# One transformer layer on one NeuronCore: the first steps in a hand-written order

## The chip, the core and the metric

The kernel runs on one core of a Trainium2 chip. The core has five engines that run their own instruction queues, each in order: TensorE (PE in the profile, with its weight loads as PEld), VectorE (DVE), ScalarE (ACT), GpSimd (POOL, here "Pool") and SyncE (SP), which here only starts transfers. They wait for each other with semaphores. The metric is the device time of one execution in microseconds (us); less is better.

## What is computed

One decoder layer for 256 tokens of width 1024, all float32. The input is normalised; one combined projection `w_in` feeds an RWKV-7 branch, a block-sparse attention branch and the gates; the branches are merged, projected, and a gated feed-forward part with a short convolution follows.

```python
h = rms_norm(x, norm1_g[l])
proj = h @ w_in[l]
z_rwkv = z_rwkv + rwkv_mu[l] * (shift_right(z_rwkv) - z_rwkv)
y_a = rwkv7_time_mix(z_rwkv, ...)
q = partial_rope(rms_norm(q, q_norm_g[l]), positions)
y_b = moba_attention(q, k, v)
x = x + (g_a * u_a + g_b * u_b) @ w_out[l]
x = x + conv_ffn(h2, w_ffn_up[l], ffn_conv_w[l], ffn_conv_b[l], w_ffn_down[l])
```

Only the first lines matter here: `rms_norm`, the first columns of `w_in` and what the first transfers bring.

## The kernel before

**Products in two parts.** Every float32 matrix is split in a high part, rounded to a format in which TensorE takes one pass (float32r), and the low rest. A product is high x high + high x low + low x high, three passes. For the weights, `load_next` (L234) starts the transfer of a block of 128 x 1024 numbers into one of four `raw` buffers, `split_hi` (L246 on ScalarE, L248 on VectorE) makes `whi` in one of four buffers, and `split_lo` (L256, VectorE) makes `wlo` in one of three and, since `raw` is then free, calls `load_next` for the next block. `wst` (L284 to L289) consumes a block: for each of two column halves eight products with `whi` (with hh and hl in turn) and four with `wlo`. For the activations hh and hl are the same two parts of the normalised input, turned so that the channels lie on the partitions.

**Who sets the order.** Instructions are written in program order, and a scheduler places those of each engine by its own estimate of when their data are there, so an instruction can stand far ahead of its place in the text. Two things bind it: `issue_after` (after a named instruction), and, in the changed kernel, `manual_schedule` (the instructions of the named engines keep the written order among themselves). Within an engine the built order is fixed: an instruction that waits holds up all behind it. Transfers are started from two queues, SP's and Pool's; each has a small number of completion semaphores that it uses in turn, so that a transfer can also wait for an earlier one of its queue.

**The first steps.** SP starts four loads of `x` (two row blocks, two halves), four weight blocks, then the ten small loads of `p1` (L397), then reloads of `raw`. Pool starts the load of `norm1_g`, makes `jp` (column minus row) and from it `ident`, the unit matrix, then starts ten small loads (`wdu`, `wgu`, `gqk`, the positions `posi`, the convolution's parameters). TensorE runs eleven products on constants so as not to start idle (`keep_warm`, L99). For each row block `norm_t` squares and sums the two halves on ScalarE (`part`, L326), takes the root (L333) and the reciprocal (L335), multiplies the rows by it into `xn` (`first`, L336 to L340), and turns them on TensorE by a product with `ident` (`turn`, L352). `second` scales with `norm1_g`, which stands in the columns of `par`, and makes hh (L357, ScalarE) and hl (L358, VectorE) for each of eight channel blocks; hh of the two blocks that share a PSUM bank are made one after the other. VectorE makes the first weight block's high part, ScalarE and VectorE the next ones.

**What follows.** The first projection (256 columns, two weight blocks) gives `xwa` and half of `xg`, a narrow one the rest. `shift` (L426 on ScalarE, L427 on VectorE) mixes each column with its predecessor, with the parameters `omm` and `par`. ScalarE takes tanh and sigmoid of them, TensorE multiplies `xwa` with `wdu` (`ch`, L494) into PSUM banks, three of which are kept for this chain, and ScalarE makes `sg` and `av`. VectorE sums `sg` along the sequence (`L`, L507, with the constant `rst`), ScalarE takes two exponentials, squares the projected keys (`sq`, L523), and TensorE sums the squares (`pss`, L529); the reciprocal roots are spread (`rx`, L536) and turned (`prx`, L546). VectorE then makes the operands of the chunk products `pgr` (L592), whose results it masks into G (L595) with `gmask`. Next to this chain run the other projections; `SLACK` and the pairs that the generators yield decide in program order how chain and projections are interleaved. `late_consts` makes the masks and other constants on VectorE, `late_params` turns the parameters `p1` and `p2` into columns, `rope_tables` makes sine and cosine of the positions (`posf`, L204, to `trig`, L225).

## Time and profile before

| | us |
|---|---|
| median of 3 runs (438.62 to 439.71) | 438.62 |
| the profiled execution | 438.61 |
| its span from first to last instruction | 436.8 |
| TensorE busy | 425.6 |
| VectorE busy | 301.4 |
| ScalarE busy | 243.0 |
| Pool busy | 12.8 |

The 1.8 us between time and span lie before the first and behind the last instruction. A row of the profile's timeline gives the start, the duration, the engine, the line, the operation, what it writes and reads, and in brackets how long the engine was idle before and what ended that. Rows of several instructions (xN) span from the first to the last. The durations of TensorE's products overlap, so their starts tell its pace.

### The profile page before, as it was taken

How to read it: one execution, taken by the hardware profiler on the slowest of the kernel's cores; microseconds unless marked ns; L12 is line 12 of the kernel's file. 1: busy time of each engine (PE TensorE's matmuls, PEld its weight loads, DVE VectorE, ACT ScalarE, POOL GpSimd, SP SyncE). 2: the span in 40 equal slices, each digit the busy share in tenths (PEclk: the TensorE clock that was granted, in tenths of full speed). 3: DMA queues.
4: the chain of work that ended last, by engine and by line, in shares of the span. 5: the costliest groups of instructions: out<-in, count | busy, mean ns of one | idle time of the engine just before them, and what ended most of it. 6: DMA issues, size and time to landing. Idle time of an engine off the chain costs nothing.

```text
span 436.8 us, 8837 instructions
## 1 busy us (share of the span) xinstructions
PE 425.6 (97%) x3600; PEld 384.0 (88%) x3600; DVE 301.4 (69%) x545; ACT 243.0 (56%) x391; POOL 12.8 (3%) x21
## 2 busy tenths in 40 slices
PE   7799998999999999999999999999999999999996
PEld 3688996788899989799997899999999999999995
DVE  4695899698456568676796479576576576576573
ACT  6489852644375446777355378455455455465450
POOL 6000040000000000000000000000000000000000
PEclk9999999999999999999999999999999999999999
DMA  8764836543657331164556366655665656565612
GB/s 234 195 190 125 243 94 195 132 129 54 194 154 230 95 104 51 50 190 127 166 182 195 107 211 184 226 189 166 200 192 178 195 193 191 191 182 185 214 50 96
DMA packets 62189, 70.76 MB, mean 162 GB/s; under 512 B 8898, under 2 KB 52617, under 8 KB 62150
## 3 DMA queue, kind: packets, MB, share of 16 engines
q1 hardware_dynamic: 61750, 69.50, 53.1%
q0 software_dynamic: 400, 0.71, 0.6%
q8 instruction: 28, 0.46, 0.4%
q14 instruction: 11, 0.09, 0.1%
HBM read 68.76 MB, written 1.44 MB: 161 GB/s over the span
## 4 chain that ended last, share of the span: by engine, by line
PE 82%; DVE 5%; ACT 5%; DMA 4%; issue 1%; SPq 1%; DVEq 0%; ACTq 0%
PE acc L284 15%; PE acc L286 15%; PE acc L289 15%; PE acc L305 4%; PE f L1045 4%; PE f L1043 4%; PE f L1044 4%; PE acc L306 4%; PE acc L309 4%; DMA raw<-in_w_in_dram 4%; DVE wlo L256 2%; ACT whi L246 1%; PE ps L876 1%; PE pp L704 1%; PE py L720 1%
## 5 line engine op out<-in xcount | busy, mean ns | idle before, releaser
L246 ACT CAST whi<-raw 128x1024 fp32r<-128x1024 f32 x121 | 126.4, 1050 | 119.3 <-PE acc L286 52.6
L256 DVE TENSOR_TENSOR wlo<-raw,whi 128x1024 fp32r<-128x1024 f32 x125 | 152.2, 1219 | 53.1 <-PE acc L289 18.4
L284 PE MATMUL acc<-hh,whi 128*128 128x256 f32 x600 | 150.1, 284 | 1.7 <-ACT whi L246 0.8
L286 PE MATMUL acc<-hl,whi 128*128 128x256 f32 x600 | 148.7, 282 | 0.9 <-DVE hl L358 0.9
L284 PEld LDWEIGHTS acc<-hh,whi 128*128 128x128 f32 x600 | 113.1, 188 | 4.4 <-ACT hh L357 1.5
L286 PEld LDWEIGHTS acc<-hl,whi 128*128 128x128 f32 x600 | 113.1, 188 | 3.2 <-DVE hl L358 1.5
L289 PE MATMUL acc<-hh,wlo 128*128 128x256 f32 x600 | 95.1, 281 | 1.2 <-DVE wlo L256 1.2
L289 PEld LDWEIGHTS acc<-hh,wlo 128*128 128x128 f32 x600 | 80.9, 189 | 2.1 <-DVE wlo L256 2.0
L1044 PE MATMUL f<-whi,hb 128*128 128x512 f32 x80 | 31.1, 389 | 0.0
L1043 PE MATMUL f<-whi,hb 128*128 128x512 f32 x80 | 31.1, 389 | 0.0
L1045 PE MATMUL f<-wlo,hb 128*128 128x512 f32 x80 | 31.1, 389 | 0.0
L305 PE MATMUL acc<-whi,hh 128*128 128x512 f32 x48 | 20.2, 425 | 0.0
L306 PE MATMUL acc<-whi,hl 128*128 128x512 f32 x48 | 18.8, 393 | 0.0
L1058 DVE TENSOR_TENSOR an<-acc,rsb 128x512 f32<-128x512 f32 x11 | 7.6, 691 | 14.8 <-PE acc L289 13.9
L1045 PEld LDWEIGHTS f<-wlo,hb 128*128 128x128 f32 x80 | 15.0, 188 | 3.1
L1044 PEld LDWEIGHTS f<-whi,hb 128*128 128x128 f32 x80 | 15.0, 188 | 2.7
L1043 PEld LDWEIGHTS f<-whi,hb 128*128 128x128 f32 x80 | 15.0, 188 | 2.7
L1076 DVE TENSOR_TENSOR cv<-cv,acc 128x256 f32<-128x256 f32 x22 | 8.3, 418 | 11.5 <-PE acc L289 11.2
L309 PE MATMUL acc<-wlo,hh 128*128 128x512 f32 x48 | 15.0, 393 | 0.0
L1065 ACT ACTIVATE cv<-an,cpar 128x256 f32<-128x256 f32 x22 | 12.0, 594 | 1.4 <-DVE an L1058 0.4
L305 PE MATMUL acc<-whi,mh 128*128 128x512 f32 x32 | 12.8, 399 | 0.0
L306 PE MATMUL acc<-whi,ml 128*128 128x512 f32 x32 | 12.6, 395 | 0.0
(274 smaller groups left out, 566.1 us busy)
## 6 DMA issues: line engine op xcount, KB each, us to landing
raw<-in_w_ffn_up_dram SPq DMA_DIRECT2D x44, 512.0 KB
raw<-in_w_in_dram SPq DMA_DIRECT2D x43, 512.0 KB
raw<-in_w_ffn_down_dram SPq DMA_DIRECT2D x22, 512.0 KB
raw<-in_w_out_dram SPq DMA_DIRECT2D x8, 512.0 KB
x<-in_x_dram SPq DMA_DIRECT2D x8, 256.0 KB
raw<-in_w_branch_b_dram SPq DMA_DIRECT2D x4, 512.0 KB
raw<-in_w_branch_a_dram SPq DMA_DIRECT2D x4, 512.0 KB
out_dram<-o SPq DMA_DIRECT2D x3, 256.0 KB
```

Source lines behind the costliest of these rows:

```text
L246: act.copy(hi[:, :k * c], raw[:, :k * c])
L256: dve.tensor_tensor(lo[:, :n], raw[:, :n], hi[:, :n].bitcast(F32), op=OP.subtract)
L284: pe.matmul(om, wh[:, k, ms], xh[:, k0 + k], start=k0 + k + m == 0, stop=False, skip_group_check=True)
L286: pe.matmul(om, wh[:, k, ms], xl[:, k0 + k], start=False, stop=False, skip_group_check=True)
L289: pe.matmul(om, wl[:, k, ms], xh[:, k0 + k], start=False, stop=k0 + k == nk - 1 and m == n - 1, skip_group_check=True)
L305: pe.matmul(ps_[t], xh[:, K, ts], wh[:, k], start=K == 0, stop=False)
L306: pe.matmul(ps_[t], xl[:, K, ts], wh[:, k], start=False, stop=False)
L309: pe.matmul(ps_[t], xh[:, K, ts], wl[:, k], start=False, stop=K == nk - 1)
L1043: pe.matmul(fin[f], hb[:, 0, i, ts], wh[:, 0, cs], start=st, stop=False)
L1044: pe.matmul(fin[f], hb[:, 1, i, ts], wh[:, 0, cs], start=False, stop=False)
L1045: pe.matmul(fin[f], hb[:, 0, i, ts], wl[:, 0, cs], start=False, stop=False)
L1065: act.activation(cv, pm, AF.Identity, scale=cpar[:, 44 + n:45 + n], bias=cpar[:, 66 + n:67 + n])
```

## The change

The steps up to the end of the first projection are written out in one function, `first_steps`, whose instructions keep their order on TensorE, ScalarE, VectorE and Pool.

- The rows are not scaled into `xn`. A diagonal matrix `diag` = `ident` x 1/rms is made, and a product with it turns and scales the rows at once; the eight blocks go to the four PSUM banks in turn, and hh and hl are made in that order, all hh of six blocks first.
- `par` comes in two parts: `p1`, now 31 rows with `norm1_g`, `rwkv_mu` and two biases, is turned early; `p2`, 116 rows with all the rest, later, called in `chain`.
- All small loads are started from Pool's queue: the five of `p1` first, five more after the iotas, ten after the first weight block's low part.
- The first weight block comes in two transfers; its high part is made on VectorE in two halves, its low part on Pool. All later high parts are made on ScalarE (before, three were VectorE's).
- The products of the first projection go through the channel blocks with hh and hl and both column halves in the inner loop, then the low parts.
- A sigmoid of a constant is taken right after the first steps, which loads ScalarE's table early.
- The constants move from VectorE to Pool (`late_consts`); the two instructions that stay are in `masks`, called before `Xb` is set up; `rope_tables` is called in `bulk` after the projection of r.

```diff
-        HI_ENG = {i: dve for i in (4, 5, 6)}
+        p1 = t1("p1", (31, 128))
+        p2 = t1("p2", (116, 128))
+        def load_rows(p, parts):
+            at = 0
+            for r, n in parts:
+                nc.gpsimd.dma_start(p[at:at + n], r)
+                at += n
...
         def late_consts():
-            dve.tensor_scalar(gmask[:, 0:64], jl[:, 0], 0.0, None, op0=OP.is_gt)
...
+            pool.memset(rst, 1.0)
+            pool.memset(rst.rearrange("p (c i) -> p c i", i=64)[:, :, 0:1], 0.0)
+            pool.memset(wgu[0:96, 1], 0.0)
+            pool.memset(bones, 0.0)
+            for q in range(2):
+                pool.memset(bones[64 * q:64 * q + 64, 64 * q:64 * q + 64], 1.0)
+            pool.tensor_scalar(gmask[:, 0:64], jl[:, 0], 0.0, None, op0=OP.is_gt)
+            pool.tensor_scalar(gmask[:, 64:128], jl[:, 1], 0.0, None, op0=OP.is_ge)
+            pool.tensor_scalar(cmask, jp, 0.0, NEG, op0=OP.is_gt, op1=OP.mult)
+            pool.memset(m16, 0.0)
+            pool.memset(m32, 0.0)
+            for q in range(4):
+                o = 32 * (q % 2)
+                pool.memset(m16[32 * q:32 * q + 32, o:o + 16], 1.0)
+                if q % 2:
+                    pool.memset(m32[32 * q:32 * q + 32, 0:32], 1.0)
+
+        def masks():
             dve.tensor_reduce(rowf, ident.rearrange("p (a b c) -> p a b c", a=4, b=2)[:, :, 1, :],
                               axis=AX.XY, op=OP.add)
...
             dve.tensor_scalar(m16, m16, rowf, None, op0=OP.mult)
...
+        def first_loads():
+            load_rows(p1, ((rows(norm1_g, 8), 8), (mu1[0:1792].rearrange("(n c) -> n c", c=128), 14),
+                           (mu1[1696:1824].rearrange("(n c) -> n c", c=128), 1),
+                           (rows(decay_bias, 4), 4), (rows(aaa_bias, 4), 4)))
+        loads = [(wdu[0:64], w_decay_up[0]), (wdu[64:128], w_aaa_up[0])]
...
+        loads.append((posi, positions[0].rearrange("(t p) -> p t", p=128)))
+        def small_loads(n):
+            for _ in range(n):
+                nc.gpsimd.dma_start(*loads.pop(0))
...
+                for ks in ((slice(0, 2), slice(2, 4)) if first else (slice(0, k),)):
+                    nc.sync.dma_start(rv[:, ks], ap[:, ks])
...
+        def first_steps():
+            for i in range(NRAW):
+                load_next(i == 0)
+            dve.memset(ones, 1.0)
...
+            keep_warm(8)
+            first_loads()
+            pool.iota(jp, pattern=[[1, 128]], base=0, channel_multiplier=-1)
+            pool.tensor_scalar(ident, jp, 0.0, None, op0=OP.is_equal)
+            for q in range(2):
+                pool.iota(jl[64 * q:64 * q + 64], pattern=[[0, 2], [1, 64]], base=0, channel_multiplier=-1)
+            small_loads(5)
+            act.activation(warm, eps1[:, 0:1], AF.Sqrt)
...
+            for t in range(2):
+                for hf in range(2):
+                    act.activation(b2("junk", [128, 512]), x_sb[t][:, hf * 512:hf * 512 + 512], AF.Square,
+                                   accum_out=ss[:, t, hf:hf + 1])
...
+                act.activation(rs[:, t:t + 1], ss[:, t, 1:2], AF.Sqrt, scale=1.0 / D, bias=ss[:, t, 0:1])
+                dve.reciprocal(rs[:, t:t + 1], rs[:, t:t + 1])
+                diag = t1("diag", (128, 128))
+                dve.tensor_scalar(diag, ident, rs[:, t:t + 1], None, op0=OP.mult)
+                for k in (0, 2, 1, 3, 4, 6, 5, 7):
+                    pe.matmul(at(k)[:, t], x_sb[t][:, k * 128:k * 128 + 128], diag, start=True, stop=True)
+                if t == 0:
+                    pt = atp("pt")
+                    pe.transpose(pt[:, 0:31], p1, ident[:31, :31])
+                    early_params(pt)
+                    keep_warm(2)
...
+            for k in range(6):
+                high(k)
+            for k in range(2):
+                dve.tensor_copy(hi[:, k * 512:k * 512 + 512], raw[:, k * 512:k * 512 + 512])
+                low(k)
+            split_lo(pool)
+            small_loads(len(loads))
+            split_hi()
+            high(6)
+            high(7)
+            for k in range(2, 8):
+                low(k)
+            split_lo()
+            split_hi()
+            p = acc()
+            for b in range(2):
+                w, wl = ready.pop(0)
...
+            split_lo()
+            dve.tensor_scalar(omm, par[:, MU:MU + 15], -1.0, 1.0, op0=OP.mult, op1=OP.add)
+            act.activation(warm, eps1[:, 0:1], AF.Sigmoid)
+            split_hi()
+            return p
+        with tc.manual_schedule(engines={E.PE, E.Activation, E.DVE, E.Pool}):
+            p = first_steps()
+        late_consts()
...
+            late_params()
             act.activation(xg[:, 0], xg[:, 0], AF.Sigmoid)
...
+            masks()
             Xb = b2("Xb", [128, 2, 16, 16])
...
             yield from proj4("r", 0)
+            rope_tables()
             yield from proj4("v", 8)
```

## The prediction

> **What bounds the kernel now.** I read the page's busy times first, then the chain of work that ended last, then TensorE's waits after the first 20 us, then busy time by stretch.

> ```profile
> span 436.8 us, 8837 instructions
> PE 425.6 (97%) x3600; PEld 384.0 (88%) x3600; DVE 301.4 (69%) x545; ACT 243.0 (56%) x391; POOL 12.8 (3%) x21
> PE 82%; DVE 5%; ACT 5%; DMA 4%; issue 1%; SPq 1%; DVEq 0%; ACTq 0%
> PE pgr L592 <- DVE G L595: 1.1, 1, 1.1
> PE acc L284 <- ACT whi L246: 0.8, 1, 0.8
> 30.00:40.00 10.00, 10.00 (x90) 10.00 (x89) 5.62 (x8) 9.92 (x16) 0.00 (x0) 1.00 0.68 207
> ```

> The columns of the last row are TensorE, its weight loads, VectorE, ScalarE and Pool, then clock and DMA. TensorE is 97% busy and 82% of the chain. After 20 us its longest waits are 1.1 and 0.8 us, and from the first group `pgr` on the instruction order is the same in both kernels. So the question is how late or early TensorE stands when the orders meet, near 73 us; the rest carries that difference to the end. Two facts limit it there. From 30 to 40 us ScalarE is full (9.92 of 10), so TensorE's lead is worth nothing if ScalarE is later. And at the start little is done: 48 products of the first projection, at four in 0.63 us, need at most 7.6 us but take 10.08 to 21.1. The marks of the kernel before:

> ```profile
> 10.08 0.35 PE L284 MATMUL acc<-hh,whi 128*128 128x256 f32 x1 [0.67 <-ACT hh L357]
> 20.46 0.63 PE L289 MATMUL acc<-hh,wlo 128*128 128x256 f32 x4
> 29.47 0.39 PE L284 MATMUL acc<-hh,whi 128*128 128x256 f32 x1
> 26.84 0.42 ACT L503 ACTIVATE xg<-xg 128x256 f32<-128x256 f32 x1 [0.69 <-DVE xg L427]
> 45.40 0.52 ACT L523 ACTIVATE sq<-zk,par 128x256 f32<-128x256 f32 x1
> 46.69 1.17 PE L529 MATMUL pss<-bones,sq 128*128 128x2 f32 x10
> 17.93 42.39 SPq L234 DMA_DIRECT2D raw<-in_w_in_dram  x15
> ```

> **The change part by part.** The normalised copies `xn` go away (a diagonal matrix of 1/rms turns and scales in one product), ten small loads leave SP's queue, the constants go from VectorE to Pool, one of ScalarE's table loads goes, three high parts (VectorE's, 0.69 us) become ScalarE's (1.05 us), and the first low part becomes Pool's. In the built instruction order of the changed kernel, though, VectorE's queue has this (a row's number is its place):

> ```
> 8 L371 TensorScalarPtr diag_152<-ident_81,rs1_140 128x128
> 9 L142 TensorScalarPtr m16_87<-m16_87,rowf_86 128x64 [waits Pool]
> 10 L152 TensorCopy par_91<-pt_162 128x31 [waits PE]
> ...
> 30 L432 TensorScalarPtr xg_301<-acc_225,par_91,xg_301 128x255
> 31 L196 TensorCopy posf_682<-posi_98 128x2 [waits the load of posi]
> 33 L246 TensorTensor wlo_395<-raw_221,whi_359 128x1024
> 34 L432 TensorScalarPtr xg_301<-acc_307,par_91,xg_301 128x255
> ```

> `masks()` and `rope_tables()`, called later in the text, were put early by the scheduler. VectorE works in order, so two waits arise.

> *First wait, for Pool's masks.* Row 9 waits for the last memset of `m16`. Pool does before it: five loads of `p1`, iota, memset of `rst`, `ident`, two iotas, five more loads, then ten memsets and three casts. Behind row 9 stand `par`, the second half's 1/rms and its diagonal, so the turned rows, hh, hl and TensorE.

> ```profile
> 1.26 0.71 POOL L89 DMA_DIRECT2D p<-in_norm_g_dram  x1 [0.82 <-POOLq L1113]
> 2.07 0.26 POOL L103 IOTA jp<- 128x128 int32 x1
> 2.47 0.58 POOL L105 TENSOR_SCALAR ident<-jp 128x128 f32<-128x128 int32 x1
> 3.31 0.62 POOL L188 DMA_DIRECT2D wdu<-in_w_decay_up_dram  x1
> 6.14 0.67 POOL L192 MEMSET wgu<- 96x512 f32 x1
> 62.09 1.82 POOL L619 MEMSET X<- 128x2048 f32 x1
> 0.24 0.10 POOL L1113 MEMSET const-float32-0.0<- 128x1 f32 x1 [0.24 <-issue]
> ```

> Five loads from 3.31 to 6.14 make 0.57 us a load. So: loads until 1.26 + 0.71 + 4 x 0.57 = 4.25; iota 4.35; `rst` (0.67 has its bytes, 1.82 twice its elements; I take 0.9) 4.55 to 5.45; `ident` and two iotas until 6.5; five loads until 9.35. Memsets by columns between 0.10 (1), 0.67 (512): `wgu` 0.67, `bones` 0.24 and 2 x 0.17, `m16` and `m32` 2 x 0.17, `rst` 0.10, four small ones 0.48; the casts, by `ident`'s 0.58 for 128 columns, 0.58 and 2 x 0.43. Together 3.6: **Pool is through at 12.9**. Bounds: 11.8 if every other memset costs the 0.10 and every cast half of `ident`'s, 15.6 if every memset of 64 columns or more costs `wgu`'s 0.67 and every cast 0.58. I stay near the low one, since the three rows fall with the columns.

> From there by the rows of before:

> ```profile
> 20.54 0.25 DVE L152 TENSOR_SCALAR m<-m,rowf 128x64 f32<-128x64 f32 x1
> 7.02 0.13 DVE L329 TENSOR_SCALAR ss<-ss 128x1 f32<-128x1 f32 x1
> 7.25 0.29 ACT L333 ACTIVATE rs<-ss 128x1 f32<-128x1 f32 x1 [0.17 <-DVE par L404]
> 7.58 0.16 DVE L335 RECIPROCAL rs<-rs 128x1 f32<-128x1 f32 x1 [0.35 <-ACT rs L333]
> 8.32 1.09 PE L352 MATMUL xt<-ident,xn 128*128 128x128 f32 x8 [0.37 <-DVE xn L336]
> 8.79 0.84 ACT L357 ACTIVATE hh<-xt,par 128x256 fp32r<-128x256 f32 x2 [0.29 <-PE xt L352]
> ```

> Mask 0.25, `par` 0.15, sum 0.13, root 0.3, reciprocal 0.2, diagonal 0.22: +1.25. First bank turned and hh: +0.5 (8.32 to 8.79), 14.65 instead of 8.79. Then hh 0.45, hl 0.45, second half of the high part 0.4: it is whole at 12.9 + 3.05 = 16.0. The five loads of `p1` are issued by 3.7 and land, at 3.7 to 7.9 us by the rows below, by 11.6: they cost nothing.

> *The low part on Pool.* Nearest rows, with VectorE's price first:

> ```profile
> 58.67 1.22 DVE L256 TENSOR_TENSOR wlo<-raw,whi 128x1024 fp32r<-128x1024 f32 x1
> 58.91 3.25 POOL L572 TENSOR_TENSOR KB<-av,L 128x1024 f32<-128x1024 f32 x1 [47.51 <-DVE av L570]
> 60.31 2.92 DVE L574 TENSOR_TENSOR KB<-kp,L 64x1024 f32<-64x1024 f32 x1
> 48.47 1.21 DVE L574 TENSOR_TENSOR KB<-kp,L 64x1024 f32<-64x1024 f32 x1
> ```

> Pool's product ends at 62.16; counted from the end of VectorE's `wlo` (59.89) it is 2.27. So 2.27 to 3.25; I take 2.6: done at 18.6. [...]

> Only then is the first raw buffer free: its reload is issued at 18.6, against 17.93 before (behind ten small loads). So SP's shorter queue gains nothing. First projection done about 22.3 (before 21.1), and with the reload's 4.2 us below, ScalarE's next high part starts at 22.8, with xwa behind it; TensorE's second group `ch` would wait from 29.1.

> *Second wait, for the positions.* Row 31 waits for `posi`, the last of ten loads that stand behind the low part on Pool: issued at 18.6 + 9 x 0.57 = 23.7.

> ```profile
> p<-in_norm_g_dram POOLq DMA_DIRECT2D x1, 4.0 KB, 3.7
> posi<-in_positions_dram POOLq DMA_DIRECT2D x1, 1.0 KB, 6.4
> wgu<-in_w_gate_up_dram POOLq DMA_DIRECT2D x1, 256.0 KB, 7.9
> 25.03 4.18 DMA raw<-in_w_in_dram
> ```

> Landing 3.7 to 7.9 us; I take 5.0, below `posi`'s own 6.4, as less of the weights is outstanding than at 10 us: **P = 28.7**. VectorE comes there at about 26.3. Behind it: memset 0.3, `wlo` 1.2, xg 0.45, so ScalarE's sigmoid of xg starts at P + 2.0 = 30.7 instead of 26.84. TensorE's second `ch` needs a bank that ScalarE reads after that sigmoid and a high part: about P + 4.5 = 33.2, and its next weights start at 34 instead of 29.47.

> *To the end.* From that sigmoid to the end of the last `sq` ScalarE, full, took 26.84 to 45.92 = 19.1; changed, the stretch has the same instructions and one more high part (+0.95): 28.7 + 2.0 + 20.0 = 50.7, 4.8 late. The run of `pss` ended 1.9 after it (47.86), as TensorE came later than its data; now it waits for them and ends about 0.5 after, at 51.2: **3.4 late**. Up to `prx` TensorE's work is otherwise equal, `rx` comes in time, and VectorE's run to G starts as late, with three products more before G and one KB fewer. I take no absorption in the 1.1 wait at G (bounds 1.1 less, 0.5 more). Sum: 438.6 of the profiled run, equal to the median, + 3.4 = **442.0**. A us of P is a us at the end, so the difference is nil at P = 25.3.

> **The rivals.** *Pool and its loads quick* (the other side): Pool through at 11.8, low part 2.27, `posi` in 3.7: P = 11.8 + 3.1 + 2.3 + 5.1 + 3.7 = 26.0, late by 0.7; with all of the G wait absorbed 0.4 early: 438.2 to 439.3. It decides at P = 25.3. For it: the tiny first load took 3.7, and Pool's memsets are unmeasured at these sizes. Against: all of Pool's later loads took 6.4 or more.

> *The positions land as late as `wgu`*: 7.9 instead of 5.0, P = 31.6, +6.3: 444.9. For it: `posi` is written in 4-byte pieces and follows 320 KB of `wgu` on its queue, and weights are reloaded then. Against: its own 6.4.

> **How the numbers follow.** Forecast 0.58 (own range 440 to 444), quick Pool 0.24, late positions 0.18. About 0.3% (1.3 us) is what a measurement of this kernel can tell from no change. The quick case splits into faster (0.11: also the 0.8 wait must go) and within 0.3% (0.13); the rest is slower, 0.76. The range goes from just under the quick case's 438.2, 438.0, to 446, 1.1 beyond the late one for masks at Pool's high bound.

> **What would show it.** Right: VectorE idle until about 13 before L142 of the changed kernel, released by Pool; first product of the projection at about 15; VectorE idle again at L196 until near 29, released by `posi`; last `sq` near 50.7. Wrong: L142 before 11.8 or L196 without a wait; TensorE making up the delay after 75 us; SP's first reload well before 18.

## The result and the profile after

| | before | after |
|---|---|---|
| device time, median (4 runs each) | 438.62 us | 445.29 us |
| lowest to highest | 438.12 to 439.71 | 444.24 to 445.98 |
| profiled execution, its span | 438.61, 436.8 | 444.24, 442.2 |
| granted clock, mean of that execution | 1.000 | 0.991 |

After to before is 1.0151, 95% interval [1.0131, 1.0172]: 6.7 us slower between medians, 5.4 us between the spans of the profiled executions. The other three runs of after had a granted clock of 0.988.

From the page of the changed kernel: busy times and the chain that ended last by engine. TensorE is 97% busy as before and now 90% of the chain. The busy time itself has grown by 4.0 us (425.6 before); the idle time grew by 1.4 (11.2 before, 12.6 now).

```profile
span 442.2 us, 8887 instructions
...
PE 429.6 (97%) x3614; PEld 390.0 (88%) x3614; DVE 296.2 (67%) x525; ACT 244.2 (55%) x393; POOL 23.9 (5%) x48
...
PE 90%; DVE 2%; ACT 2%; DMA 2%; issue 0%; DVEq 0%; POOL 0%; ACTq 0%
```

The two waits of VectorE that the instruction order had shown, in its timeline:

```profile
12.25 0.25 DVE L142 TENSOR_SCALAR m<-m,rowf 128x64 f32<-128x64 f32 x1 [6.01 <-POOL m L135]
13.28 0.29 DVE L371 TENSOR_SCALAR diag<-ident,rs 128x128 f32<-128x128 f32 x1
...
31.20 0.17 DVE L196 CAST posf<-posi 128x2 f32<-128x2 int32 x1 [4.18 <-DMA posi<-in_positions_dram]
```

Both are there: 6.0 us for Pool's masks, 4.2 us for the positions. TensorE's timeline and its waits from 5 to 100 us show what it stood for:

```profile
13.62 3.38 PE L373 MATMUL xt<-diag,x 128*128 128x128 f32 x16 [2.57 <-DVE diag L371]
16.65 0.78 PE L411 MATMUL acc<-hh,whi 128*128 128x256 f32 x2
33.13 1.13 PE L497 MATMUL ch<-xwa,wdu 64*128 64x256 f32 x6 [2.17 <-ACT sg L503]
50.79 1.17 PE L533 MATMUL pss<-bones,sq 128*128 128x2 f32 x10
```
```profile
PE xt L373 <- DVE diag L371: 3.8, 2, 2.6
PE ch L497 <- ACT sg L503: 2.2, 1, 2.2
PE pgr L596 <- DVE G L599: 0.7, 1, 0.7
PE acc L415 <- POOL wlo L246: 0.5, 1, 0.5
```

TensorE's 2.57 us before the second row block stand behind the masks; in e1 below, which takes that wait away, 0.86 of them are left. The 2.17 us before the second `ch` are not the positions'. ScalarE's timeline, and the piece of the chain of waits that ends at 30.90:

```profile
28.80 0.40 ACT L507 ACTIVATE xg<-xg 128x256 f32<-128x256 f32 x1
30.93 1.05 ACT L236 CAST whi<-raw 128x1024 fp32r<-128x1024 f32 x1 [1.73 <-DMA raw<-in_w_in_dram]
31.88 0.47 ACT L503 ACTIVATE sg<-ch,par 128x256 f32<-128x256 f32 x1
33.31 0.43 ACT L508 ACTIVATE xg<-xg 128x256 f32<-128x256 f32 x1
49.33 0.91 ACT L527 ACTIVATE sq<-zk,par 128x256 f32<-128x256 f32 x2
```
```profile
22.81 8.09 DMA raw<-in_w_in_dram
```

The sigmoid of the first half of `xg` (L507) ran at 28.80, before the positions had landed; only the second half (L508) stands behind them. `sg` stands behind a high part (30.93) whose reload took 8.09 us instead of the 4.18 quoted of before. It was issued among ten small loads, with the first reload at 19.58; that they made it slow is an assumption.

So far this explains the idle time. The busy time is in the busy times by stretch (columns as in the prediction's row: length, TensorE, its loads, VectorE, ScalarE, Pool, granted clock, DMA). First before, then after; the cut is the start of the first `pgr`, from which the order is the same:

```profile
0.00:66.59 66.59, 60.43 (x443) 52.49 (x443) 50.39 (x112) 48.09 (x81) 12.84 (x21) 1.00 0.64 180
66.59:436.80 370.21, 365.18 (x3159) 331.55 (x3158) 250.96 (x434) 194.87 (x310) 0.00 (x0) 1.00 0.53 159
```
```profile
14.10:17.51 3.41, 3.41 (x19) 3.41 (x18) 1.31 (x4) 2.51 (x7) 0.35 (x1) 0.50 0.00 0
34.60:38.01 3.41, 3.41 (x18) 3.41 (x17) 1.77 (x5) 3.36 (x6) 0.00 (x0) 0.50 0.48 149
...
0.00:72.45 72.45, 64.52 (x457) 58.58 (x457) 46.70 (x94) 49.19 (x83) 23.87 (x48) 0.95 0.60 171
72.45:442.20 369.75, 365.12 (x3159) 331.46 (x3158) 249.48 (x433) 194.99 (x310) 0.00 (x0) 1.00 0.52 158
```

The first `pgr` is 5.86 us later, and the rest takes 0.46 less. Of the 5.86, idle time is 1.77 (7.93 against 6.16) and busy time 4.09. In two stretches of 3.41 us, 0.5 and 1.5 us after the two long pauses ended, TensorE was busy throughout at half the clock. In the second it started a product of 128x256 every 0.21 us, from 38.87 us on every 0.12. As an estimate, length times what the clock lacks of 1.00, the two cost half of 6.82, 3.41 us. The remaining 0.7 is a net that was not taken apart: 32 records of diagonal products stand where there were 16 transposes, ten constant products where there were eleven, and the first row block took 3.78 us instead of 1.48.

The same stretches, cut at the first product of the projection (10.08 and 16.65), tell where the loss lies. First before, then after, each from that product to the first `pgr`:

```profile
10.08:66.59 56.51, 52.84 (x415) 48.68 (x415) 46.54 (x92) 41.22 (x65) 5.73 (x3) 1.00 0.61 170
16.65:72.45 55.80, 53.15 (x416) 50.72 (x415) 43.69 (x73) 42.44 (x67) 12.91 (x13) 0.96 0.56 160
```

The changed kernel is 6.57 us late at that product and needs no longer than the kernel before for what follows, with the second pause and the second half clock in it. Against the kernel before, the whole loss thus stands ahead of the projection. That this stretch can be shorter, e10 below shows with 53.06 us.

### The profile page after: what moved, and what is told of

It reads as the page before. It is cut to its first block, busy times and chain, and to the rows that moved or that the text cites. A ratio compares the mean times of both kernels' runs of the same rounds, so it can differ in the third digit from the quotient of the medians.

```text
span 442.2 us, 8887 instructions
## 1 busy us (share of the span) xinstructions
PE 429.6 (97%) x3614; PEld 390.0 (88%) x3614; DVE 296.2 (67%) x525; ACT 244.2 (55%) x393; POOL 23.9 (5%) x48
## 4 chain that ended last, share of the span: by engine, by line
PE 90%; DVE 2%; ACT 2%; DMA 2%; issue 0%; DVEq 0%; POOL 0%; ACTq 0%
PE acc L274 17%; PE acc L276 17%; PE acc L279 17%; PE acc L295 4%; PE f L1049 4%; PE f L1051 4%; PE f L1050 4%; PE acc L296 4%; PE acc L299 4%; DMA raw<-in_w_in_dram 2%; PE ps L881 1%; PE pp L709 1%; DVE wlo L246 1%; PE py L725 1%; ACT whi L236 1%; PE po L918 1%
## 5 line engine op out<-in xcount | busy, mean ns | idle before, releaser
L236 ACT CAST whi<-raw 128x1024 fp32r<-128x1024 f32 x124 | 129.8, 1050 | 121.0 <-PE acc L276 55.7
L246 DVE TENSOR_TENSOR wlo<-raw,whi 128x1024 fp32r<-128x1024 f32 x124 | 152.5, 1234 | 53.0 <-PE acc L279 18.4
L274 PE MATMUL acc<-hh,whi 128*128 128x256 f32 x584 | 147.2, 286 | 0.0
L276 PE MATMUL acc<-hl,whi 128*128 128x256 f32 x584 | 145.1, 282 | 0.0
L274 PEld LDWEIGHTS acc<-hh,whi 128*128 128x128 f32 x584 | 111.0, 190 | 2.3 <-issue 1.0
L276 PEld LDWEIGHTS acc<-hl,whi 128*128 128x128 f32 x584 | 111.1, 190 | 1.1 <-issue 0.3
L279 PE MATMUL acc<-hh,wlo 128*128 128x256 f32 x584 | 92.9, 282 | 0.2 <-DVE rs L1032 0.2
L279 PEld LDWEIGHTS acc<-hh,wlo 128*128 128x128 f32 x584 | 79.3, 190 | 0.5 <-DVE wlo L246 0.4
L1082 DVE TENSOR_TENSOR cv<-cv,acc 128x256 f32<-128x256 f32 x22 | 8.3, 417 | 11.8 <-PE acc L279 11.5
L295 PE MATMUL acc<-whi,mh 128*128 128x512 f32 x32 | 12.9, 402 | 0.0
## 6 DMA issues: line engine op xcount, KB each, us to landing
x<-in_x_dram SPq DMA_DIRECT2D x8, 256.0 KB, 3.8
out_dram<-o SPq DMA_DIRECT2D x3, 256.0 KB, 2.1
```

Of the source, the lines that this page charges most:

```text
L236: act.copy(hi[:, :k * c], raw[:, :k * c])
L246: eng.tensor_tensor(lo[:, :n], raw[:, :n], hi[:, :n].bitcast(F32), op=OP.subtract)
L274: pe.matmul(om, wh[:, k, ms], xh[:, k0 + k], start=k0 + k + m == 0, stop=False, skip_group_check=True)
L276: pe.matmul(om, wh[:, k, ms], xl[:, k0 + k], start=False, stop=False, skip_group_check=True)
L279: pe.matmul(om, wl[:, k, ms], xh[:, k0 + k], start=False, stop=k0 + k == nk - 1 and m == n - 1, skip_group_check=True)
L295: pe.matmul(ps_[t], xh[:, K, ts], wh[:, k], start=K == 0, stop=False)
```

## The experiments

Five theories are weighed. Theory A: the late start makes ScalarE's chain (`sg`, `sq`) late, and that sets the end. Theory B, as predicted: the wait for the positions sets it. Theory C: the diagonal products are slow. Theory D, formed after the first four runs: what counts is TensorE's own time, its pauses and the half clock that follows them. Theory E, formed on the trace of e9: a different order behind the first `pgr` is worth time of its own.

Each ratio is to the kernel before, run beside it in five rounds (its medians were 438.5 to 439.0). For each profiled execution the table gives the start of the first `pgr`, idle and busy time until then, and the time lost to a clock below 1.00 from 5 us to that point, an estimate: stretches of 1 us, each times what its clock lacks of 1.00, summed. In e2 and e3 the clock fell to 0.50 while TensorE was still idle (at 12.9 and 18.9 us, before products at 17.71 and 21.19), so part of their figure is no lost work. These columns are one execution each, which lies up to 1.8 us from the median of its kernel (e4's took 441.48 us, e11's 440.47, e1's 444.48). And the clock column may be incomplete at the start: in e11 both row blocks, at 6.61 and 11.88, took 3.78 us with the clock shown as 1.00, and 2.05 each in e8. So a zero in the last column means that no half clock is recorded.

| kernel | median us | ratio to before, 95% | first pgr | idle | busy | lost to the clock |
|---|---|---|---|---|---|---|
| before | 438.6 | | 66.59 | 6.16 | 60.43 | 0 |
| after | 445.29 | 1.0151 [1.0131, 1.0172] | 72.45 | 7.93 | 64.52 | 3.41 |
| e1 mask product on Pool | 443.03 | 1.0106 [1.0089, 1.0123] | 72.53 | 7.31 | 65.22 | 3.41 |
| e2 positions early | 446.74 | 1.0188 [1.0170, 1.0206] | 74.78 | 11.23 | 63.55 | 5.12 |
| e3 small loads first | 446.53 | 1.0195 [1.0171, 1.0219] | 73.84 | 11.71 | 62.13 | 3.42 |
| e4 low part on VectorE | 439.70 | 1.0031 [1.0010, 1.0052] | 68.94 | 7.39 | 61.55 | 0 |
| e5 = e1 + filled pause | 444.13 | 1.0113 [1.0087, 1.0138] | 70.71 | 6.22 | 64.49 | 1.70 |
| e6 = after + filled pauses | 449.57 | 1.0236 [1.0213, 1.0259] | 75.36 | 9.19 | 66.17 | 3.41 |
| e7 high parts on VectorE | 446.45 | 1.0166 [1.0138, 1.0194] | 74.99 | 7.74 | 67.25 | 8.54 |
| e8 = e4 + e7 | 443.91 | 1.0109 [1.0074, 1.0143] | 71.07 | 7.15 | 63.92 | 5.12 |
| e9 TensorE's order alone | 439.46 | 1.0009 [0.9997, 1.0020] | 72.79 | 8.36 | 64.43 | 1.71 |
| e10 = e4 + pss later | 439.20 | 1.0000 [0.9983, 1.0017] | 66.13 | 4.69 | 61.44 | 0 |
| e11 = e8 + pss later | 438.80 | 1.0004 [0.9989, 1.0019] | 68.03 | 4.92 | 63.11 | 0 |
| e12 = e10 + fuller start | 439.26 | 1.0014 [1.0003, 1.0025] | 67.34 | 5.33 | 62.01 | 0 |

**e1: the mask product on Pool.**

```diff
-            dve.tensor_scalar(m16, m16, rowf, None, op0=OP.mult)
+            pool.tensor_scalar(m16, m16, rowf, None, op0=OP.mult)
```

> The product of m16 by rowf is moved from VectorE to Pool, so VectorE no longer waits for Pool's masks at its ninth instruction; the wait for the positions stays. Theory A (the late start sets the end: all reloads and the ten small loads bunch at 19.6 to 25 us, one reload takes 8 us, ScalarE in order behind it): the second diagonal is ready about 2 us earlier (11.3 instead of 13.3), everything behind shifts by that, time 442.3 to 444.3. Theory B (the wait for the positions sets the end): the time follows the landing of the positions one to one, with VectorE's wait for them as long as before, 443 to 445. Theory C (the start is late because the diagonal products themselves are slow at a cold clock): less than 0.7 us gained, 444.6 to 445.5.

443.03 us, as A said, and just within B; C falls. The second diagonal came at 11.28, and the last `sq` ended at 47.1 instead of 50.2. Yet in the profiled execution, the slowest of the five, the first `pgr` is no earlier: the half clock had moved. TensorE's waits and one stretch of e1:

```profile
PE pss L533 <- ACT sq L527: 1.8, 2, 1.6
```
```profile
47.60:54.42 6.82, 6.82 (x35) 6.82 (x34) 3.04 (x4) 2.90 (x5) 0.00 (x0) 0.50 0.61 191
```

TensorE, earlier than `sq` now, waited 1.6 us for it and then ran 6.82 us at half clock. From here on ScalarE's lateness alone could not be the account.

**e2: the positions early.**

```diff
-        loads = [(wdu[0:64], w_decay_up[0]), (wdu[64:128], w_aaa_up[0])]
+        loads = [(posi, positions[0].rearrange("(t p) -> p t", p=128)),
+                 (wdu[0:64], w_decay_up[0]), (wdu[64:128], w_aaa_up[0])]
...
-        loads.append((posi, positions[0].rearrange("(t p) -> p t", p=128)))
```

> The load of the positions goes to the front of the second batch of small loads, about 13 us earlier on its queue (r_k goes to the third batch in exchange). The cast of the positions then stands on VectorE ahead of the m16 product, with the angle operations behind it. Theory A: no gain, and a loss as far as the cast or the angles hold up the second row block at the start by 1 to 3 us: 445 to 448. Theory B: the wait at 27 to 31 us is gone and with it 3 us or more: 440 to 442.5. Theory C: as now, 445.

446.74 us, as A said. The wait at 31 us is gone and the time rose by 1.5 us, since the planner now put the cast and the angle operations ahead of the second row block. VectorE's and TensorE's timelines:

```profile
12.72 0.17 DVE L196 CAST posf<-posi 128x2 f32<-128x2 int32 x1 [6.49 <-DMA posi<-in_positions_dram]
```
```profile
17.71 3.79 PE L373 MATMUL xt<-diag,x 128*128 128x128 f32 x16 [7.13 <-DVE diag L371]
```

```profile
36.84 1.13 PE L497 MATMUL ch<-xwa,wdu 64*128 64x256 f32 x6 [1.41 <-ACT sg L503]
```

The start is 4.1 us later than after's (17.71 against 13.62), so the time alone doesn't refute B. The second `ch` speaks against it: it is 3.7 us later (36.84 against 33.13), so if all else moves with the start, the positions' wait was worth 0.4 us there. And the start that was 4.1 late cost 1.5 at the end.

**e3: the small loads ahead of the low part.**

```diff
-            split_lo(pool)
             small_loads(len(loads))
+            split_lo(pool)
```

> The ten late small loads stand ahead of the first low part on Pool, so they are issued at about 9 to 14 us, while no weight is being loaded, and the masks come after them. Theory A: the reloads then have the DMA engines to themselves and the one of 8.1 us takes 4 to 5; TensorE's wait of 2.2 us for sg and its stretch at half pace go, unless the low part becomes later: 441 to 443. Theory B: the positions land by about 20 us, the wait is gone: 440 to 442.5. Theory C: as now, 444.5 to 445.5.

446.53 us, against all three. The low part itself became late and TensorE waited for it:

```profile
21.19 2.08 PE L415 MATMUL acc<-hh,wlo 128*128 128x256 f32 x8 [5.38 <-POOL wlo L246]
```

Pool had stood in the middle of the loads; its row for the ninth load of the group that begins with `wdu`, issued when the first of them had landed:

```profile
13.08 0.55 POOL L189 DMA_DIRECT2D p<-in_ffn_conv_w_dram  x1 [2.49 <-DMA wdu<-in_w_decay_up_dram]
```

What the bunching of loads costs is not told by this run.

**e4: the first low part on VectorE.** The planner then puts the ten loads ahead of Pool's memsets and the mask product far back, so mask wait, Pool's low part and positions' wait all go.

```diff
-            split_lo(pool)
+            split_lo()
```

> The first low part is made by VectorE instead of Pool; in the built order the ten late loads then come ahead of Pool's memsets and the m16 product goes far back on VectorE, so both waits change place. Theory A: start about 2 us earlier, first raw buffer free at about 16 instead of 19.6, no bunching: 439.5 to 442. Theory B: positions early, 440 to 442.5. Theory C: the diagonal products stay cold and slow, 444 to 445.5.

439.70 us, as A said and a little below B. No stretch at half clock in the profiled execution, although e1 and e4 are alike in ScalarE's chain (last `sq` ended at 47.1 and 47.0). That pair led to theory D: 443.0 and 439.7 with the same `sq`.

**e5 and e6: constant products in the pauses.** e5 is e1 with 16 of them ahead of `pss`; e6 is the changed kernel with seven more between the row blocks and 20 ahead of the second `ch`.

```diff
             p = chp("pss")
+            for _ in range(16):
+                pe.matmul(p[:, 256:512], ones[:, 0:128], ones[:, 0:256], start=True, stop=True)
```
```diff
-                    keep_warm(2)
+                    keep_warm(9)
...
                 pw = [chp() for _ in range(2)]
+                if j == 1:
+                    for _ in range(20):
+                        pe.matmul(pw[0][:, 0:256], ones[:, 0:128], ones[:, 0:256], start=True, stop=True)
```

> The kernel with the mask product on Pool, and 16 products of the constant ones into an unused part of the bank of pss, put on TensorE ahead of the pss products, so in the pause of 1.6 us that came just before the clock was halved there (granted clock 0.50 from 47.2 to 54.3 us). Theory D (short pauses of TensorE cost more than themselves, since the granted clock is halved for 3 to 7 us after them): the clock stays at 1.00, prx comes about 3 us earlier, time 439.5 to 440.5 instead of 443.0. Theory A (only the lateness of ScalarE's chain counts): unchanged or up to 0.5 us worse, 443 to 443.5.

> The changed kernel with TensorE kept busy in its two pauses: nine instead of two constant products between the row blocks (pause of 2.6 us at 11.0) and 20 constant products ahead of the second group of ch (pause of 2.2 us at 31.0). Waits and loads stay as they are. Theory D: both stretches at half clock (14.5 to 17.8 and 34.2 to 38.0 us) go, worth about 1.5 and 1.8 us: 442 to 443.5 instead of 445.3. Theory A: the waits of ScalarE for the reloads set the end, less than 1 us gained: 444.3 to 445.3.

444.13 and 449.57 us: both miss. In e5 the filled pause was followed by no half clock, but the pause before the second `ch` was 1.69 us there (0.81 in e1) and 3.41 us at half clock followed that. Its six runs have clocks of 0.995 (two, mean 442.4) and 0.992 (four, mean 444.6). In e6 only the second place was filled: the nine constant products ahead of the second row block were over at 10.59, and a pause of 3.08 us followed. No half clock came behind either place; it came after 50 us, behind two pauses at `pss` of 1.4 and 0.9 us, and again after 80 us (clock 0.91 from 80 to 100). Filling one pause didn't help while the next stayed, and the filling is work in TensorE's own queue. Why e6 is 4.3 us slower than the changed kernel was not taken apart.

**e7 and e8: the fourth to sixth high part on VectorE**, in the changed kernel and in e4.

```diff
+        nhi = [0]
+
-        def split_hi(eng=act):
+        def split_hi(eng=None):
             if raws:
+                nhi[0] += 1
+                eng = eng or (dve if nhi[0] in (4, 5, 6) else act)
```

> The changed kernel with the fourth to sixth high part back on VectorE, as before the change. In the built order sg no longer stands behind a high part on ScalarE that waits for its reload, and the load of the sine table moves behind the last sq. Theory A: sg 1.5 to 3 us earlier, last sq at 46.5 to 48.5 instead of 50.2, time 441 to 443.5. Theory B (the wait for the positions): they hold VectorE as before, no gain, 445. Theory D alone: no gain unless the pause before the second ch becomes shorter.

> Both: the first low part on VectorE (with the small loads ahead of the masks and the mask product late, as in the run with that edit alone) and the fourth to sixth high part on VectorE. Theory A: the gains of both add, last sq at 44 to 46, time 436.5 to 438.5, below the kernel before. If VectorE becomes the bound instead: 439 to 441.

446.45 and 443.91 us, where A had 441 to 443.5 and 436.5 to 438.5: A falls here. e7's last `sq` ended at 48.8, 1.4 us before that of the changed kernel, and its first `pgr` starts 2.5 us later, with 8.54 us lost to the clock. e8's last `sq` ended at 44.75, 1.2 us before that of the kernel before and 5.5 before that of the changed one, and it is 5 us slower than the former. What its early ScalarE made of TensorE: three pauses at `pss`, as `sq` came one by one.

```profile
41.44 0.35 PE L537 MATMUL pss<-bones,sq 128*128 128x2 f32 x2 [0.60 <-ACT sq L531]
42.69 0.38 PE L537 MATMUL pss<-bones,sq 128*128 128x2 f32 x2 [0.90 <-ACT sq L531]
43.45 0.59 PE L537 MATMUL pss<-bones,sq 128*128 128x2 f32 x2 [0.38 <-ACT sq L531]
```

**e9, e10, e11: TensorE's order.** Only numbers of the planner change, by which the `pss` products (and in e9 the second `ch`) come later in TensorE's queue; e10 is e4 and e11 is e8 with the last two changes.

```diff
-                yield 0.9, 0.8
+                yield 0.9, 2.0
...
-            yield 0, 1.5
+            yield 0, 2.5
...
-            yield 0.5, 2.0
+            yield 0.5, 0.5
```

> The changed kernel with nothing moved but TensorE's order: the second group of ch and the pss products stand one block of four weights (1.4 us) further back each, prx half a us earlier in the planner. All loads, both waits of VectorE and ScalarE's work stay. Theory D (the granted clock, halved after short pauses of TensorE, carries most of the loss): the pause of 2.2 us before the second ch shrinks to 0.8 or less, the half-clock stretch from 34.2 to 38.0 goes, the one at the start stays: 441 to 443. Theory A (the lateness of ScalarE's chain carries it): sg and sq are as late as before or 1 us later, 445 to 446.

> The kernel with the first low part on VectorE, with the pss products two blocks (2.8 us) further back on TensorE, so that TensorE does not wait 1.3 us for sq. Theory D: its clock is at 0.998 or more in most runs already, so it gains at most the pause: 438.5 to 440, and the rare runs at 0.992 go. Theory A: prx one block later costs up to 1.4 us: 440 to 441.5.

> The kernel with the first low part and the fourth to sixth high part on VectorE, with the pss products two blocks (2.8 us) further back on TensorE: its three pauses at pss (0.6, 0.9 and 0.4 us within 2.6 us), after which the clock was at 0.50 from 43.3 to 53.7 us, go. Theory D: clock 0.995 or more, 438 to 440 instead of 443.9. If only the pauses themselves count: 1.9 us less at most, 442 to 443.9.

439.46, 439.20 and 438.80 us. For e9 both theories miss (D had 441 to 443, A 445 to 446); e10 and e11 are as D said in time (clocks of 0.995 or more, which D gave e11, were not reached in all its runs). The clean pair is e8 and e11: 443.91 and 438.80 us, one edit, the same order from the first `pgr` on. They were not run beside each other, but each beside the kernel before, and their ratios to it (1.0109 and 1.0004) are 4.6 us apart. The pauses alone had been put at 1.9 us, for 442 us or more. First e8, then e11: the busy times of the stretch that was at half clock in e8, and the last `sq` from ScalarE's timeline.

```profile
43.30:53.54 10.24, 10.09 (x47) 10.09 (x48) 5.65 (x7) 5.66 (x9) 0.00 (x0) 0.50 0.51 146
```
```profile
44.23 0.52 ACT L531 ACTIVATE sq<-zk,par 128x256 f32<-128x256 f32 x1
```
```profile
43.30:53.54 10.24, 9.68 (x86) 9.59 (x85) 10.05 (x15) 10.18 (x17) 0.00 (x0) 1.00 0.55 155
```
```profile
46.47 0.52 ACT L531 ACTIVATE sq<-zk,par 128x256 f32<-128x256 f32 x1
```

TensorE is "busy" for 10.09 of 10.24 us in e8 and gets 47 products started; in e11, with `sq` 2.2 us later, it is busy for less and starts 86. The start of this execution of e11 was slow (the row blocks at 3.78 us), so the kernels are compared from the first product `acc` behind the projection to the first `pgr`. First e8, then e11:

```profile
19.86:71.07 51.21, 49.34 (x367) 47.21 (x365) 39.55 (x64) 32.43 (x54) 8.50 (x14) 0.90 0.55 155
```
```profile
22.11:68.03 45.92, 44.90 (x368) 42.82 (x366) 39.76 (x65) 32.28 (x54) 4.97 (x2) 1.00 0.61 173
```

For the same number of products e8 takes 5.29 us more, 0.85 of them idle and 4.44 busy, at a mean clock of 0.90 against 1.00. This shows D: a later `sq` and a faster kernel, and more lost to the slow pace than to the pauses themselves.

e9 looks like the stronger proof and is not. Its ScalarE chain and both waits of VectorE are as late as in the changed kernel (`sg` at 31.92, positions at 30.59, mask at 12.16), and it is 5.8 us faster. But the row of the first `pz`, of after and then of e9, and e9's time from its first `pgr`:

```profile
93.81 1.15 PE L663 MATMUL pz<-VU,G 64*64 64x64 f32 x32
```
```profile
93.44 1.15 PE L663 MATMUL pz<-VU,G 64*64 64x64 f32 x32
```
```profile
72.79:437.90 365.11, 361.03 (x3153) 328.94 (x3152) 247.57 (x430) 194.00 (x309) 0.00 (x0) 1.00 0.53 159
```

At 94 us e9 leads by only 0.4 us; 4.3 lie between the spans. The number for the second `ch` also moved bulk products in the planner's order after 94 us, and 3.9 us were gained there. This gain belongs to the new order (E), not to the first steps. Whether it adds to e10, or comes in the kernel before as well, was not tried.

**e12: a fuller start**: e10 with `keep_warm(11)` instead of 8, and `low(2)`, `low(3)` ahead of the first low part.

> The kernel with the first low part on VectorE and the pss products two blocks back, with two things more at the start: eleven instead of eight constant products ahead of the first row block, and two more hl ahead of the first low part on VectorE. What is asked is whether anything at the start is still worth time once TensorE's order is mended. Theory D: the first row block takes 2.05 instead of 3.4 to 3.8 us and TensorE's pause of 0.8 us for hl goes; half of that is lost again at the parameters' load, which lands at about 9 us: 437.8 to 438.8, a little below the kernel before. If the start is hidden from here on: as the kernel without these edits, 439.2.

439.26 us, no gain, as said for a start that is hidden (439.2). The first row block took 2.05 us, but so it did in e3, e6 and e8 without this edit. The first product of the projection started 1.0 us earlier than in e10 (12.09 against 13.07), but a pause of 1.89 us for `xwa` followed at 24.28. Between 439.70 (e4), 439.20 (e10) and 439.26 (e12) the intervals overlap. No version here beats the kernel before; e9, e10 and e11 equal it.

## Why the prediction was right and where it was not

Slower was forecast, and 442.0 us with a range to 446.0; it is 445.29. The direction and the whole range held. The size did not: 3.4 us were forecast and 6.7 measured, outside the 440 to 444 of the forecast's own case. Point by point:

- *What counts is how late TensorE is at the first `pgr`*: right, in the profiled execution. 5.86 us late there, 0.46 made up behind it, at the G wait (0.66 instead of 1.10) as the bound had it.
- *First wait, Pool through at 12.9*: right, 12.25. Pool's first ten loads were issued by 9.01 (estimated 9.35), and the memset of `wgu` took 0.54 (0.67).
- *From there to the projection at about 15*: the diagonal (13.28) and the first hh (14.48, forecast 14.65) came in time, the projection at 16.65. The term that was missing is the pace: the second row block took 3.38 us, as the clock fell to 0.50 at 14.10; the same block took 2.05 in e1 and e4. So TensorE was 6.57 us late here, where the forecast's 15 is 4.9, and nearly all of it was still there at the first `pgr`; the prediction had let this lateness vanish in the wait for ScalarE.
- *Low part on Pool 2.6*: 2.40, between the low bound of 2.27 and the 2.6 taken. The bound counts Pool's product from the end of an instruction of VectorE; that Pool waits for such an end was assumed, and no run shows it. First reload at 19.58 (forecast 18.6), by the delay of the row block.
- *Second wait, P = 28.7*: the wait was there and longer (31.2; the load took 6.8 us from issue), but what hangs on it was wrong, and this is the step that failed first. "ScalarE's sigmoid of xg starts at P + 2.0" holds for the second half of `xg` only; the first half did not wait. The second `ch` came at 33.13 and the next weights at 34.18, nearly the forecast 33.2 and 34, through another chain: the reload of 8.09 us, the high part behind it, and `sg` behind that. In e2, without this wait, the second `ch` came 3.7 us later behind a start 4.1 later.
- *Last `sq` at 50.7*: 50.24. Right in size, as the two chains happened to be as long.
- *To the end: +3.4 as `pss` is 3.4 late and "TensorE's work is otherwise equal"*: the other step that failed. TensorE's work was equal, its pace was not. e8 and e11 show that the end does not follow `sq` at all within some 2 us: it follows what TensorE gets done. By the profiled execution the sum is 1.8 more idle, 3.4 at half clock, 0.7 more busy for other reasons, less 0.46: 5.4. The rest of the 6.7 between medians goes with the clock of the other runs of after (0.988 against 0.991, one stretch of 3.41 us more by its size); there is no trace of them, so this is argued. A lower mean clock does not always cost that much: of the kernel before, five runs at 0.988 average 440.0 us and four at 1.000 average 438.7.
- *The rivals*: quick Pool did not occur. "Positions as late as `wgu`" gave 444.9 and lies near the result by luck: its positions came nearly so late (31.2 against its 31.6), but what it hung on them did not follow.
- The signs named ahead (idle before L142 and L196, `sq` near 50.7) all appeared, and the mechanism was wrong all the same: they tested that the waits exist, not that the end depends on them.

What stays open: how much of e4's gain is the mask wait and how much Pool's low part (e1 takes the mask wait alone away, 2.3 us, but with a half clock in another place); what the bunching of the reloads costs by itself; and what decides whether the clock is halved behind a pause and for how long. That pauses and slow pace carry the loss is shown on e8 and e11; for the changed kernel itself it is read from its trace, since e9, which left its start as it was, brought a new order with it.

## What to carry to other kernels

Where TensorE is the bound, split its time at a point of equal order into idle and busy, and compare busy with the granted clock, before following a chain on another engine: here two pauses of 2 to 3 us were each followed by 3.41 us at half clock (1.7 us lost, by the estimate above), and 4.1 of 5.9 us of delay were in time that counts as busy. An engine that gets its data ready sooner can go with a slower kernel if TensorE's queue puts the consumer too early (e8 against e4: last `sq` 2 us earlier, 443.91 against 439.70 us); here it helped to move the consumer back behind work that was ready, and it did not help to fill the pause. A sign named ahead should test the consequence (what starts late, and by how much) and not only that the wait is there.

## What was not expected of the hardware

```profile
18.31 2.61 POOL L128 TENSOR_SCALAR gmask<-jl 128x64 f32<-128x64 int32 x1
```
```profile
9.77 0.39 POOL L128 TENSOR_SCALAR gmask<-jl 128x64 f32<-128x64 int32 x1
```
